# Scaling the residual rows on GpSimd during the up projections, and loading the second half's rows early

## The chip, the cores and the metric

The kernel runs on one NeuronCore of a Trainium2 chip. Its engines work side by side, each through its own queue in order, and wait for one another by semaphores: TensorE (PE in the profile: matrix products, with PEld for the loading of the stationary operand), VectorE (DVE), ScalarE (ACT), GpSimd (POOL) and SyncE (SP, which here only issues transfers). A name with a q (SPq, POOLq) is the queue of an engine, which starts its transfers. The metric is the time of one execution on the device, in microseconds; lower is better.

## The reference

Two layers of a small language-model trunk over a sequence of 1024 tokens of width 1024, in float32. Each layer has a mixer (in the first a gated delta rule, in the second a retention) and a feed-forward part with a gate, and each of the two ends in a residual sum and a layer norm:

```
for i in range(DEPTH):                       # DEPTH = 2
    mod = (e @ ada_w[i] + ada_b[i])[:, None, :]
    sh1, sc1, g1, sh2, sc2, g2 = jnp.split(mod, 6, axis=-1)
    y = mixers[i % N_MIXERS](x * (1.0 + sc1) + sh1)
    x = layer_norm(DN_ALPHA * x + (1.0 + g1) * y, ln_g[i, 0], ln_b[i, 0])
    y = conv_ffn(x * (1.0 + sc2) + sh2, ffn_up[i], ffn_conv_w[i], ffn_conv_b[i], ffn_down[i])
    x = layer_norm(DN_ALPHA * x + (1.0 + g2) * y, ln_g[i, 1], ln_b[i, 1])
return x
```

`e` comes from a conditioning vector. `conv_ffn` has an up projection to twice 2816 columns, a short causal convolution and a gate, and a down projection back to 1024.

What matters for the change: a layer norm is a normalization per row, then a multiplication by a row `ln_g` and the addition of a row `ln_b` (the gain). The sum in front of the second norm needs the first norm's output with its gain.

## The kernel before, in words

*Layout.* A tile has 128 partitions; a row tile holds 128 tokens with 1024 columns (or 512, a half, `HALF`). The sequence is worked on in two halves of 512 tokens, four row tiles each. Matrices are split into a high and a low part (`split`, L88 to L90: ScalarE rounds, VectorE subtracts) and multiplied by three products. Large products use a seven-product scheme over blocks of two by two.

*Rows.* The norm in the middle of a layer writes normalized rows without the gain to a tensor in DRAM, `x_mid` (`xs`); the stores are on ACT's queue (`ln_store`, L372 to L374). The products behind the norm have the gain folded into their scale and shift (`fold`). The residual sum at the layer's end needs the rows with the gain.

*The stages of one layer's end* (`layer_tail`, L1519): in the first layer a projection with norm (`proj_ln`, which loads the layer's input rows `xt<-in_x`, L284); in the second one a seven-product projection (`proj_gen`) does that. Then come the up projections (`strassen`, L1161): 22 items, the first two by a plain scheme (`side`), during which the operands' sums are built (`build_T`, L411, with the transposes of L425 that read the second half's rows), and 20 by seven products (`wino`, L1220). `wino` loads two weight tiles (`wr<-in_ffn_up`, L1223 and L1224), each item about 19 us of TensorE, and calls `bg_step` twice. `bg_step` works off a list of background units: here the products of the conditioning (`bg_ada`: a load `mvw<-in_ada_w`, L215, and behind it multiply-adds on VectorE into `ada`, L225 and L227). The results of a pair of items are stored as `ad<-o` (L1573), partly after sums on GpSimd (L1589). Last is the down projection, again `proj_gen` (L1278): seven products in the order of `prods`, each over `nj` blocks, with loads `ar<-ad` (L1274) and `Br<-in_ffn_down` (L1307) on SP, and results worked off by f1 to f7 and by `finish` and `norm`.

*The gain for the residual rows of the down projection* is made inside `proj_gen`, two ways. For the first half `xload` (L1352) loads the rows without gain in the third product (p == 2), and VectorE multiplies and adds (L1357). For the second half `gain_half` (L1343) does one half row tile in every other step of the fourth and fifth product (p of 3 and 4): SP loads it into one of two buffers with the tag `xT`, GpSimd multiplies and adds (L1349), and a transfer on GpSimd's own queue (L1350) stores it to `xg[i + 1]`. The second half's rows are loaded from there behind the sixth product's work, into the same four `lane` buffers that the first half's rows had. `load_row` waits by `after("w")` for the issue of the last weight block.

*Buffers.* Tags name sets of equal buffers (`BUFS`, L43): `lane` 4, `xT` 2, `auh` 8 of half width (gain rows, gate rows, later trigonometric tables `trig`, L1636), `wr` 2. A tile's load waits until the buffer's last use has ended.

*Order of the work.* The program is written as one stream; a scheduler with a simulated timeline puts each engine's instructions in their order when the program is built. An engine's queue is then worked off strictly in that order: a transfer that waits at the head of SP's queue holds all behind it.

Of the kernel before, what the change touches and what calls it, by code (L numbers as in the profile page):

```python
# [15 lines left out]
P = 128  # L16
# [3 lines left out]
HALF = 512  # L20
# [13 lines left out]
def trunk_kernel(ctx: ExitStack, tc, A):  # L34
# [84 lines left out]
    def bg_step(tile=mm_tile):  # L119
        bg_ps[0] = tile  # L120
        for p in pend:
            p[0] -= 1
        while pend and (pend[0][0] <= 0 or not bg):
            pend.pop(0)[1]()
            if not bg:
                break
        if bg:
            nxt = bg.pop(0)()
            if nxt:
                pend.append(list(nxt))  # L130

    def gemm_feat(src, hT_, step=True):
# [247 lines left out]

    def bg_gain(n, src, dst):
        gb = []

        def unit(c, r):
            if r == 0:
                gb[:] = [tl("auh", [P, HALF], name="gb") for _ in range(2)]
                for t, nm in zip(gb, ("ln_g", "ln_b")):
                    sp.dma_start(t, A[nm][n:n + 1, hs(c)].to_broadcast([P, HALF]))
            x = tl("lane", [P, HALF], name="xg")
            rs = slice(r * P, r * P + P)  # L390
            sp.dma_start(x, src[rs, hs(c)])
            if r == 7:
                return gain(x, rs, c)
            return 1, lambda: gain(x, rs, c)

        def gain(x, rs, c):
            pool.tensor_tensor(x, x, gb[0], ALU.mult)
            pool.tensor_tensor(x, x, gb[1], ALU.add)
            sp.dma_start(dst[rs, hs(c)], x)

        for c in range(2):
            for r in range(8):
                bg.append(lambda c=c, r=r: unit(c, r))

# [756 lines left out]
    def strassen(hT0, xts, scale, shift, items, tags=("hTb", "hTb", "qkv", "qkv", "aux"), direct=False):  # L1161
# [58 lines left out]
        def wino(n, sink):  # L1220
# [27 lines left out]
            sink(2, prod(a22, "T4"), u3)  # L1248
            bg_step()

        bg_tag[0] = "lane"
# [25 lines left out]

    def proj_gen(nj, ablk, wsrc, slots, xsrc, G, final, ln_next, tag, ltags, dst, key, mm=pe.matmul, gate=None, gain=None):  # L1278
        bal = {nm: BAL[ltags[4] + nm] for nm in ABLK + ("w11", "w21", "w22", "wT1", "wT2", "wT3", "wT4", "n", "h")}
# [60 lines left out]
        stats = [[], []]  # L1340
        grows = gain_rows(gain[0], key) if gain else None

        def gain_half(n):  # L1343
            hf, rs = n // 4, slice(HALF + n % 4 * P, HALF + (n % 4 + 1) * P)
            x = tl("xT", [P, HALF], name="xg")
            with after("w"):
                sp.dma_start(x, gain[1][rs, hs(hf)])
            for r, op in zip(grows, (ALU.mult, ALU.add)):
                pool.tensor_tensor(x, x, r[hf], op)  # L1349
            pool.dma_start(xsrc[rs, hs(hf)], x)  # L1350

        def xload(half, t):  # L1352
            xt = load_row(xsrc if half or not gain else gain[1], half, t)
            if half == 0 and gain:
                for r, op in zip(grows, (ALU.mult, ALU.add)):
                    for hf in range(2):
                        dve.tensor_tensor(xt[:, hs(hf)], xt[:, hs(hf)], r[hf], op)  # L1357
            xts[half].append(xt)
            stats[half].append(tl("st", [P, 2, 6]))

        def finish(half, t, nh, c):
            dve.tensor_tensor(c, c, G[nh], ALU.mult)
            xv = xts[half][t][:, hs(nh)]
            dve.scalar_tensor_tensor(xv, xv, ALPHA, c, ALU.mult, ALU.add)
            dve.bn_stats(stats[half][t][:, nh], xv)

        def norm(half, t):
# [7 lines left out]
            else:  # L1375
                (gB, bB), out = final
                r0 = half * HALF + t * P
                dve.scalar_tensor_tensor(mv[:, 2:3], mv[:, 0:1], -1.0, mv[:, 3:4], ALU.mult, ALU.mult)
                lo, hi = xt[:, hs(0)], xt[:, hs(1)]
                act.activation(hi, hi, AF.Identity, bias=mv[:, 2:3], scale=mv[:, 3:4])  # L1380
# [70 lines left out]
        for p, (an, bn, fin, side, fresh) in enumerate(prods):  # L1451
# [8 lines left out]
            for j in range(nj):  # L1460
# [5 lines left out]
                with after("a"):  # L1466
                    for st in steps[p * nj + j + ahead:p * nj + j + ahead + 1]:
                        load_b(*st)
                if gain and p in (3, 4) and j % 2 == 0 and j < 8:
                    gain_half((p - 3) * 4 + j // 2)  # L1470
                if gain and p == 2 and j % 2 == 0 and j < 8:
                    xload(0, j // 2)
                if p == 2 and j < 4 and gate:
                    xload(0, j)
# [29 lines left out]
            if p == 4:  # L1504
                hooks = [] if final else ln_hooks(0, xts[0], tag, ln_next, outs, dst, key, bal["h"])
                hooks += [lambda t=t: xload(1, t) for t in range(4)]
        if not final:
# [11 lines left out]
    def layer_tail(i, mix, wout, xsrc, x_mid, x_out, ln_next, final):  # L1519
# [11 lines left out]
        else:  # L1531
            mix.append((sc2, sh2))
            hT0, xts = proj_st(mix[0])
        bg_ada(i, 5, "row")
        if i == 0:
            for j in (1, 0, 4, 3):
# [6 lines left out]
        def pair_items(fp):  # L1543
# [31 lines left out]
            def up_start():  # L1575
                seen = []

                def gated(q, a, b):
# [7 lines left out]
                    if len(seen) == 4:  # L1586
# [7 lines left out]

        strassen(hT0, xts, sc2, sh2, [it for fp in range(NF // 2) for it in pair_items(fp)])
        slots = {"c": "hTa", "x": "qkv"}
        gb2 = gain_rows(3, ("mid", i), "hTb") if final else None
        return proj_st(proj_gen(NF // 2, ablk_of(ad, "qkv"), A["ffn_down"][i], slots, xg[i + 1], rows[i, 5],
                       (gb2, x_out) if final else None, ln_next, "hTb", ("hTb", "hTa", 8, 6, "f") if final else ("qkv", "hTa", 8, 4, "0"), x_out, ("out", i), gain=(2 * i, x_mid)))

# [357 lines left out]
```

## Time and profile before

Three runs took 2961.66, 2965.21 and 2967.01 us, median 2965.21. The profiled execution took 2955.5 us; its span (first to last instruction) is 2953.7 us, at a granted TensorE clock of 0.984.

| stretch (us) | what | PE busy | DVE busy | POOL busy | granted clock |
|---|---|---|---|---|---|
| 645 to 760 | first layer, projection with norm | 109.10 of 115 | 78.12 | 8.58 | 0.97 |
| 760 to 1195 | first layer, up projections | 428.39 of 435 | 367.73 | 50.28 | 0.99 |
| 1195 to 1425 | first layer, down projection | 218.38 of 230 | 192.87 | 47.19 | 0.99 |
| 2100 to 2290 | second layer, end of the mixer and its projection | 176.93 of 190 | 155.45 | 32.43 | 0.96 |
| 2290 to 2717 | second layer, up projections | 418.74 of 427 | 325.20 | 49.37 | 1.00 |
| 2717 to 2953 | second layer, down projection, end | 215.15 of 236 | 207.55 | 50.19 | 0.97 |

How to read it: "busy" is the time in which an engine worked on instructions; the rest it waited or had nothing to do. PE is the engine that is busy most, so the columns of the others matter where PE is below the stretch's length. The granted clock is the share of full speed that TensorE was given.

### The profile page before, as it was taken

Reading aid. Unit: us, or ns where it says so; the run is one execution under the profiler, and the core shown is the slowest. Engines: PE = TensorE matmul, PEld = TensorE weight load, DVE = VectorE, ACT = ScalarE, POOL = GpSimd, SP = SyncE. Lnnn points to the kernel's source line nnn. Section 1 sums busy time; section 2 is a strip of 40 time slices with the busy share of each in tenths; the row PEclk is TensorE's granted clock in tenths of the full one; section 3 lists DMA queues with packets and bytes.
Section 4 is the critical chain, followed back from the end, with each engine's and each line's share of the span. In section 5 each row is a group of like instructions: output and inputs, shape, how many; then the busy total and the mean of one; then the engine's idle time right before and its main releaser. Section 6 shows DMA issues by size and latency. Waiting matters only on the chain.

```text
span 2953.7 us, 38896 instructions
## 1 busy us (share of the span) xinstructions
PE 2816.4 (95%) x13638; PEld 2303.2 (78%) x13638; DVE 2243.3 (76%) x4005; ACT 1318.0 (45%) x2413; POOL 451.1 (15%) x469
## 2 busy tenths in 40 slices
PE   8998898999999999999999999999999899999997
PEld 7887777887788888877878877777777788888885
DVE  5788787656688888968676756666689787777989
ACT  4745565444544444545333333222244544445443
POOL 0302221100001111140000022422202011111211
PEclk9999999999999999999999999999999999999999
DMA  7231222254244445765343364755654343324763
GB/s 277 86 111 65 83 79 80 83 168 158 92 160 163 150 162 174 286 225 175 131 147 121 109 229 144 222 169 177 198 204 146 103 136 107 107 102 159 278 205 136
DMA packets 244403, 451.01 MB, mean 153 GB/s; under 512 B 23088, under 2 KB 76592, under 8 KB 244208
## 3 DMA queue, kind: packets, MB, share of 16 engines
q1 hardware_dynamic: 213088, 401.07, 41.1%
q10 hardware_dynamic: 29760, 43.00, 4.0%
q0 software_dynamic: 1360, 4.46, 0.4%
q8 instruction: 107, 1.75, 0.2%
q14 instruction: 88, 0.72, 0.1%
HBM read 339.91 MB, written 108.53 MB: 152 GB/s over the span
## 4 chain that ended last, share of the span: by engine, by line
PE 77%; DVE 9%; DMA 6%; ACT 4%; issue 2%; POOL 1%; SPq 0%; POOLq 0%; ACTq 0%; DVEq 0%
PE acc L655 15%; PE acc L1167 10%; PE acc L110 6%; PE acc L111 6%; PE acc L112 6%; PE sc L1167 5%; PE acc L1441 4%; PE sc L655 4%; PE mm L655 2%; PE sc L111 2%; PE sc L112 2%; PE sc L110 2%; PE mm L658 1%; DMA Br<-in_ffn_down 1%; PE acc L314 1%
## 5 line engine op out<-in xcount | busy, mean ns | idle before, releaser
L655 PE MATMUL acc<-hT,wh 128*128 128x512 f32 x960 | 300.1, 394 | 0.0
L1441 PE MATMUL acc<-bb,ab 128*128 128x512 f32 x984 | 233.4, 395 | 9.7 <-DVE bb L90 7.0
L1589 POOL TENSOR_TENSOR o<-o 128x512 f32<-128x512 f32 x80 | 112.3, 1414 | 793.6 <-DVE o L1582 494.0
L1441 PEld LDWEIGHTS acc<-bb,ab 128*128 128x128 f32 x984 | 183.7, 189 | 54.0 <-DVE bb L90 11.8
L1167 PE MATMUL acc<-T,wb 128*128 128x512 f32 x840 | 202.9, 390 | 6.5 <-DVE wb L90 6.5
L655 PEld LDWEIGHTS acc<-hT,wh 128*128 128x128 f32 x960 | 182.2, 190 | 34.1
L89 ACT ACTIVATE ab<-ar 128x512 fp32r<-128x512 f32 x210 | 130.4, 627 | 174.1 <-PE mm L291 57.4
L655 PE MATMUL acc<-hT,wl 128*128 128x512 f32 x480 | 201.2, 419 | 0.0
L1167 PEld LDWEIGHTS acc<-T,wb 128*128 128x128 f32 x840 | 157.0, 188 | 42.9 <-DVE wb L90 9.8
L90 DVE TENSOR_TENSOR wl<-wr,wh 128x1024 fp32r<-128x1024 f32 x95 | 123.3, 1298 | 81.9 <-ACT wh L89 81.6
L90 DVE TENSOR_TENSOR ab<-ar,ab 128x512 fp32r<-128x512 f32 x210 | 159.7, 765 | 30.0 <-ACT ab L89 29.9
L90 DVE TENSOR_TENSOR wb<-mm,wb 128x512 fp32r<-128x512 f32 x216 | 146.0, 684 | 26.4 <-ACT wb L89 25.5
L89 ACT ACTIVATE wh<-wr 128x1024 fp32r<-128x1024 f32 x95 | 100.8, 1062 | 142.8 <-PE acc L655 66.4
L90 DVE TENSOR_TENSOR wb<-wr,wb 128x512 fp32r<-128x512 f32 x162 | 110.5, 687 | 69.0 <-ACT wb L89 68.8
L1228 ACT ACTIVATE pc<-acc 128x512 f32<-128x512 f32 x143 | 84.9, 594 | 163.1 <-PE acc L1167 108.8
L1568 DVE SCALAR_TENSOR_TENSOR o<-g,vc,o 128x512 f32<-128x512 f32 (+2 forms) x176 | 145.6, 844 | 6.2 <-ACT o L1563 5.5
L89 ACT ACTIVATE wb<-mm 128x512 fp32r<-128x512 f32 x216 | 123.9, 595 | 53.8 <-DVE mm L1217 49.3
L89 ACT ACTIVATE wb<-wr 128x512 fp32r<-128x512 f32 x162 | 99.8, 629 | 99.7 <-DMA wr<-in_ffn_up 36.4
L655 PE MATMUL acc<-wh,hT 128*128 128x512 f32 x384 | 137.4, 420 | 2.9 <-DVE vv L90 1.7
L110 PE MATMUL acc<-T,wb 128*128 128x512 f32 x292 | 115.6, 396 | 9.4 <-DVE wb L90 9.4
L476 DVE SCALAR_TENSOR_TENSOR qkv<-raw,vc,qkv 128x512 f32<-128x512 f32 x144 | 111.7, 780 | 11.4 <-ACT qkv L474 10.7
L111 PE MATMUL acc<-T,wb 128*128 128x512 f32 x292 | 115.1, 394 | 0.0
(641 smaller groups left out, 7428.6 us busy)
## 6 DMA issues: line engine op xcount, KB each, us to landing
wr<-in_ffn_up SPq DMA_DIRECT2D x92, 512.0 KB, 4.2
mvw<-in_ada_w SPq DMA_DIRECT2D x80, 512.0 KB, 4.1
ad<-o SPq DMA_DIRECT2D x154, 256.0 KB, 3.1
ar<-ad SPq DMA_DIRECT2D x154, 256.0 KB, 4.8
Br<-in_ffn_down SPq DMA_DIRECT2D x88, 256.0 KB, 4.3
wr<-in_ret_wv SPq DMA_DIRECT2D x32, 512.0 KB, 4.1
ar<-od SPq DMA_DIRECT2D x56, 256.0 KB, 5.4
xs<-xt ACTq DMA_DIRECT2D x24, 512.0 KB, 3.6
```

The costliest lines, as they stand in the source:

```text
L89: act.activation(dst_h, src, AF.Copy)
L90: eng.tensor_tensor(dst_l, src, dst_h, ALU.subtract)
L110: mm(acc, wl[:, k], hl[0], start=first, stop=False)
L111: mm(acc, wh[:, k], hl[1], start=False, stop=False)
L112: mm(acc, wh[:, k], hl[0], start=False, stop=last)
L476: dve.scalar_tensor_tensor(oh, raw[:, 3 - j:515 - j], w[:, 3 - j:4 - j], oh, ALU.mult, ALU.add)
L655: pq(pe.matmul(out, lhsT, rhs, start=start, stop=stop), cost)
L1167: return pe.matmul(*a, skip_group_check=True, **kw)
L1228: act.activation(t, X, AF.Copy)
L1441: return pe.matmul(*args, skip_group_check=True, **kw)
L1568: dve.scalar_tensor_tensor(tv, gv[:, c0 - j:c1 - j], w[:, 2 - j:3 - j], tv, ALU.mult, ALU.add)
L1589: (dve if fp == 0 else pool).tensor_tensor(o[d], o[x], o[y], op)
```

## The change

Both halves' rows are now scaled by one helper, `bg_gain`, that existed for another place. For the rows of the down projections it puts 16 units (two column halves, eight row tiles each) on a list of its own, `rowq`; `row_step`, called at the end of each `wino`, finishes the unit loaded before (GpSimd multiplies and adds, and stores through its own queue) and starts the next load, into the `xT` buffers. What is left of the list is worked off behind `strassen`. `gain_half` and VectorE's multiplications and additions in `xload` go. The gain rows of one column half are two `auh` tiles where four were held before.

Second, the second half's rows: the first two row tiles go to the two `xT` buffers instead of `lane`; in the last projection (`final`) the other two go to pairs of `auh` tiles, and all four are loaded during the fourth product (p == 3). `xh` picks a column half from either kind of tile. The mixer's projection in the second layer (`gate`) has the `xT` part of this too.

```diff
--- before.py
+++ after.py
@@ -128,6 +128,16 @@
             nxt = bg.pop(0)()
             if nxt:
                 pend.append(list(nxt))
+
+    rowq, rowp = [], []
+
+    def row_step():
+        if rowp:
+            rowp.pop()()
+        if rowq:
+            nxt = rowq.pop(0)()
+            if nxt:
+                rowp.append(nxt[1])
 
     def gemm_feat(src, hT_, step=True):
         w = load_w(src)
@@ -378,7 +388,7 @@
 
     xg = [dr.tile([S, D], F32, tag=f"xg{i}", name=f"xg{i}") for i in range(3)]
 
-    def bg_gain(n, src, dst):
+    def bg_gain(n, src, dst, tag="lane"):
         gb = []
 
         def unit(c, r):
@@ -386,7 +396,7 @@
                 gb[:] = [tl("auh", [P, HALF], name="gb") for _ in range(2)]
                 for t, nm in zip(gb, ("ln_g", "ln_b")):
                     sp.dma_start(t, A[nm][n:n + 1, hs(c)].to_broadcast([P, HALF]))
-            x = tl("lane", [P, HALF], name="xg")
+            x = tl(tag, [P, HALF], name="xg")
             rs = slice(r * P, r * P + P)
             sp.dma_start(x, src[rs, hs(c)])
             if r == 7:
@@ -396,11 +406,11 @@
         def gain(x, rs, c):
             pool.tensor_tensor(x, x, gb[0], ALU.mult)
             pool.tensor_tensor(x, x, gb[1], ALU.add)
-            sp.dma_start(dst[rs, hs(c)], x)
+            (sp if tag == "lane" else pool).dma_start(dst[rs, hs(c)], x)
 
         for c in range(2):
             for r in range(8):
-                bg.append(lambda c=c, r=r: unit(c, r))
+                (bg if tag == "lane" else rowq).append(lambda c=c, r=r: unit(c, r))
 
     def ln_hooks(half, xts, tag, vecs2, out, dst, key, npool=0):
         def build(f):
@@ -1247,6 +1257,7 @@
             sink(3, X, z5)
             sink(2, prod(a22, "T4"), u3)
             bg_step()
+            row_step()
 
         bg_tag[0] = "lane"
         for n in range(2):
@@ -1275,7 +1286,7 @@
             return raw
         return ablk
 
-    def proj_gen(nj, ablk, wsrc, slots, xsrc, G, final, ln_next, tag, ltags, dst, key, mm=pe.matmul, gate=None, gain=None):
+    def proj_gen(nj, ablk, wsrc, slots, xsrc, G, final, ln_next, tag, ltags, dst, key, mm=pe.matmul, gate=None):
         bal = {nm: BAL[ltags[4] + nm] for nm in ABLK + ("w11", "w21", "w22", "wT1", "wT2", "wT3", "wT4", "n", "h")}
         pa = [tl("aux", [P, 2, HALF], name="pa") for _ in range(4)]
         p1 = [pa[t // 2][:, t % 2] for t in range(4)]
@@ -1338,29 +1349,28 @@
 
         xts = [[], []]
         stats = [[], []]
-        grows = gain_rows(gain[0], key) if gain else None
-
-        def gain_half(n):
-            hf, rs = n // 4, slice(HALF + n % 4 * P, HALF + (n % 4 + 1) * P)
-            x = tl("xT", [P, HALF], name="xg")
-            with after("w"):
-                sp.dma_start(x, gain[1][rs, hs(hf)])
-            for r, op in zip(grows, (ALU.mult, ALU.add)):
-                pool.tensor_tensor(x, x, r[hf], op)
-            pool.dma_start(xsrc[rs, hs(hf)], x)
 
         def xload(half, t):
-            xt = load_row(xsrc if half or not gain else gain[1], half, t)
-            if half == 0 and gain:
-                for r, op in zip(grows, (ALU.mult, ALU.add)):
-                    for hf in range(2):
-                        dve.tensor_tensor(xt[:, hs(hf)], xt[:, hs(hf)], r[hf], op)
-            xts[half].append(xt)
+            if half and t < 2:
+                x = load_row(xsrc, half, t, tag="xT")
+            elif half and final:
+                x = two("auh", F32, "xt")
+                r0 = HALF + t * P
+                for hf in range(2):
+                    with after("w"):
+                        sp.dma_start(x[hf], xsrc[r0:r0 + P, hs(hf)])
+            else:
+                x = load_row(xsrc, half, t)
+            xts[half].append(x)
             stats[half].append(tl("st", [P, 2, 6]))
+
+        def xh(half, t, nh):
+            x = xts[half][t]
+            return x[nh] if isinstance(x, tuple) else x[:, hs(nh)]
 
         def finish(half, t, nh, c):
             dve.tensor_tensor(c, c, G[nh], ALU.mult)
-            xv = xts[half][t][:, hs(nh)]
+            xv = xh(half, t, nh)
             dve.scalar_tensor_tensor(xv, xv, ALPHA, c, ALU.mult, ALU.add)
             dve.bn_stats(stats[half][t][:, nh], xv)
 
@@ -1376,7 +1386,7 @@
                 (gB, bB), out = final
                 r0 = half * HALF + t * P
                 dve.scalar_tensor_tensor(mv[:, 2:3], mv[:, 0:1], -1.0, mv[:, 3:4], ALU.mult, ALU.mult)
-                lo, hi = xt[:, hs(0)], xt[:, hs(1)]
+                lo, hi = xh(half, t, 0), xh(half, t, 1)
                 act.activation(hi, hi, AF.Identity, bias=mv[:, 2:3], scale=mv[:, 3:4])
                 dve.scalar_tensor_tensor(lo, lo, mv[:, 0:1], gB[0], ALU.subtract, ALU.mult)
                 dve.scalar_tensor_tensor(lo, lo, mv[:, 3:4], bB[0], ALU.mult, ALU.add)
@@ -1466,10 +1476,10 @@
                 with after("a"):
                     for st in steps[p * nj + j + ahead:p * nj + j + ahead + 1]:
                         load_b(*st)
-                if gain and p in (3, 4) and j % 2 == 0 and j < 8:
-                    gain_half((p - 3) * 4 + j // 2)
-                if gain and p == 2 and j % 2 == 0 and j < 8:
+                if not gate and p == 2 and j % 2 == 0 and j < 8:
                     xload(0, j // 2)
+                if final and p == 3 and j % 2 == 0 and j < 8:
+                    xload(1, j // 2)
                 if p == 2 and j < 4 and gate:
                     xload(0, j)
                     finish(0, j, 0, c11[j])
@@ -1503,7 +1513,8 @@
                 yield "P2"
             if p == 4:
                 hooks = [] if final else ln_hooks(0, xts[0], tag, ln_next, outs, dst, key, bal["h"])
-                hooks += [lambda t=t: xload(1, t) for t in range(4)]
+                if not final:
+                    hooks += [lambda t=t: xload(1, t) for t in range(4)]
         if not final:
             for t in range(4):
                 ln_store(1, t, xts[1], dst, key)
@@ -1532,6 +1543,7 @@
             mix.append((sc2, sh2))
             hT0, xts = proj_st(mix[0])
         bg_ada(i, 5, "row")
+        bg_gain(2 * i, x_mid, xg[i + 1], "xT")
         if i == 0:
             for j in (1, 0, 4, 3):
                 bg_ada(1, j, "col")
@@ -1593,10 +1605,12 @@
             return [(up[4 * fp], up[4 * fp + 2], gate_start, conv), (up[4 * fp + 1], up[4 * fp + 3], up_start, None)]
 
         strassen(hT0, xts, sc2, sh2, [it for fp in range(NF // 2) for it in pair_items(fp)])
+        while rowq or rowp:
+            row_step()
         slots = {"c": "hTa", "x": "qkv"}
         gb2 = gain_rows(3, ("mid", i), "hTb") if final else None
         return proj_st(proj_gen(NF // 2, ablk_of(ad, "qkv"), A["ffn_down"][i], slots, xg[i + 1], rows[i, 5],
-                       (gb2, x_out) if final else None, ln_next, "hTb", ("hTb", "hTa", 8, 6, "f") if final else ("qkv", "hTa", 8, 4, "0"), x_out, ("out", i), gain=(2 * i, x_mid)))
+                       (gb2, x_out) if final else None, ln_next, "hTb", ("hTb", "hTa", 8, 6, "f") if final else ("qkv", "hTa", 8, 4, "0"), x_out, ("out", i)))
 
     g1 = two("auh", F32, "g1")
     for nh in range(2):
```

## The prediction

> **What bounds the kernel now.** I read the page first (busy shares, then the forty slices), next the tensor engine's waits and busy time by stage, then the chain of waits through the worst stage, and last the timelines of the places where the change puts its work.
>
> ```profile
> span 2953.7 us, 38896 instructions
> PE 2816.4 (95%) x13638; PEld 2303.2 (78%) x13638; DVE 2243.3 (76%) x4005; ACT 1318.0 (45%) x2413; POOL 451.1 (15%) x469
> ```
>
> PE is busy 95% of the span, so work taken from another engine gains only where PE waits for it, and work put on another engine costs only where PE comes to wait. One stage where it waits is the first layer's down projection:
>
> ```profile
> 1225.00:1255.00 30.00, 30.00 (x134) 24.85 (x133) 30.00 (x51) 15.02 (x27) 1.86 (x1) 1.00 0.75 273
> 1285.00:1315.00 30.00, 30.00 (x134) 24.73 (x132) 14.13 (x17) 13.15 (x24) 13.65 (x12) 1.00 0.83 290
> 1315.00:1345.00 30.00, 23.02 (x96) 18.78 (x95) 26.95 (x45) 6.95 (x13) 0.00 (x0) 0.89 0.60 191
> ```
>
> Columns of this view: stretch, length, busy time (instructions) of PE, PEld, DVE, ACT and POOL, then granted clock, DMA share, GB/s. From 1315 PE loses 7 us, and the clock falls to 0.89. The waits of PE and the chain say why:
>
> ```profile
> PE sc L289 <- DVE u L1414: 7.0, 1, 7.0
> ```
> ```profile
> 1283.60 5.80 DMA xg<-xs
> ...
> 1292.88 3.98 DMA xg<-xg
> ...
> 1296.91 3.44 DMA xg<-xs
> ...
> 1309.54 5.14 DMA Br<-in_ffn_down
> ```
>
> The row loads of `gain_half` have two buffers. The load at 1296.91 had to wait until the store of an earlier row (1292.88, 3.98 us) had landed; it stood at the head of SP's queue, and the weight block `Br` behind it came too late. One buffer's cycle, load to next load, was 1296.91 - 1283.60 = 13.3 us here.
>
> **The change part by part.**
>
> *Removed from the down projections.* Sixteen VectorE multiplications and additions per layer (L1357) and the eight half rows of `gain_half`, each with a load on SP, two POOL operations and a store on POOL's queue.
>
> ```profile
> L1357 DVE TENSOR_TENSOR xt<-xt,rowb x32: 677/681/686, 1234.6 to 2781.2; 128x512 f32<-128x512 f32 x32
> ```
>
> 32 x 0.681 = 21.8 us leave VectorE, but where they stand (1225 to 1255 above) PE is busy 30.00 of 30: I take 0 (the cover is PE itself; without it, half of this per layer). The SP queue of the down projections no longer holds a load that waits for a buffer, so the 7.0 us wait goes, and with it the slow restart, 30 x (1 - 0.89) = 3.3 us: -10.3. Bounds: -7.0 if the clock dips elsewhere, -13 if the waits for VectorE just after it go too.
>
> *Added to the up projections: where the rows really stand.* The source puts one row behind each seven-product unit, but the built order of the changed program does not spread them. In the first layer SP's order is:
>
> ```
> xg 1, xg 2, wr, wr, xg 3, wr, xg 4, xt<-in_x x4, ... xg 5, xg 6, wr, xg 7, xg 8, trig, xg 9, trig,
> xg 10, xg 11, wr(L1223), xg 12, wr(L1224), xg 13 to 16, mvw, trig x2, ad x4, wr(L1223), ...
> ```
>
> All sixteen loads stand ahead of the first `mvw` (a block of the conditioning weights) of the up projections. In the second layer it is xg 1 to 4, the first pair's weights, xg 5 to 8, `mvw`, and the rest mixed with the second and third pairs' weights. SP takes its queue in order, and two buffers serve all rows; so whatever stands behind row n waits for row n - 2 to be loaded, scaled and stored. The price of a row, by the nearest rows:
>
> ```profile
> L1349 POOL TENSOR_TENSOR xg<-xg,rowb x32: 1280/1604/8602, 1253.1 to 2833.2; 128x512 f32<-128x512 f32 x32
> ```
> ```profile
> L1347 SPq DMA_DIRECT2D xg<-xs x16: 319/372/435, 1250.1 to 2828.1; - x16
> ...
> DMA to landing us min/median/max: 2.9/3.3/6.1
> ```
> ```profile
> L1350 POOL DMA_DIRECT2D xg<-xg x16: 559/582/759, 1263.7 to 2834.8; - x16
> ...
> DMA to landing us min/median/max: 2.4/3.2/5.4
> ```
> ```profile
> mvw<-in_ada_w SPq DMA_DIRECT2D x80, 512.0 KB, 4.1
> ...
> xs<-xt ACTq DMA_DIRECT2D x24, 512.0 KB, 3.6
> ```
>
> In the first layer POOL's order puts one operation of the partner row ahead of each store, so a cycle of a pair of rows is load 3.3 + three operations 4.8 + about 0.3 before the issue + landing 3.2 = 11.6 us. Bounds: all minima, 2.9 + 3.8 + 0.3 + 2.4 = 9.4; the cycle seen in the chain, 13.3.
>
> ```profile
> 755.57 0.33 ACTq L374 DMA_DIRECT2D xs<-xt  x1
> ```
> ```profile
> 791.30 0.38 SPq L215 DMA_DIRECT2D mvw<-in_ada_w  x1
> ```
> ```profile
> 811.01 0.48 DVE L225 TENSOR_SCALAR ada<-mvw,e 128x512 f32<-128x512 f32 x1
> ```
> ```profile
> 817.12 2.10 PE L1167 MATMUL acc<-T,wb 128*128 128x512 f32 x8 [0.49 <-DVE wb L90]
> ```
>
> Row 5 is the first of the second half: its source is stored at 755.57 and lands 3.6 us later, 759.2. Row 15 is five cycles behind, 759.2 + 58.0 = 817.2; row 16 one operation and one issue later, 819.4; then `mvw`, 819.7, which lands at 823.8. Before, `mvw` was issued at 791.30 and had long landed when VectorE read it at 811.01 (L225). VectorE's order at this place is the same in both programs, so it would stand at L225 until 823.8, 12.8 us. Behind it on VectorE are the splits (`wb`, L90) for which PE waits already at 817.12: nothing covers it, **+12.8**. Bounds by the same sum: with 9.4 us +1.8, with 13.3 us +21.3. The delay of the first pair's weights (row 11 at 794, against 788.33 before) and of the next pair's fall inside this wait.
>
> In the second layer the two buffers hold normalized rows until their last transposes:
>
> ```profile
> 2303.36 1.03 PE L425 MATMUL mm<-cst,xt 128*128 128x128 f32 x8
> ```
> ```profile
> 2319.59 0.60 SPq L215 DMA_DIRECT2D mvw<-in_ada_w  x1
> ```
> ```profile
> 2339.32 0.48 DVE L225 TENSOR_SCALAR ada<-mvw,e 128x512 f32<-128x512 f32 x1
> ```
>
> Row 1 can load at 2304.4. POOL's order here has the four operations of a pair ahead of both stores: 3.3 + 6.4 + 0.3 + 3.2 = 13.2 us a cycle (bounds 10.7 and 14.9, as above with one operation more). Row 7 loads at 2304.4 + 39.6 = 2344.0, row 8 at 2344.6, `mvw` at 2345.0, landed at 2349.1 against 2339.32: **+9.8** (bounds +2 and +15; the upper end rises by 7 if the third pair's weights, behind row 14, are late too).
>
> *The stores on POOL's queue.* 32 instead of 16, 0.58 us each on POOL, which has 85% free; inside the cycles above. The Trainium skill warns of such stores (SBUF — State Buffer, "SBUF: two separate sides"): a DMA issued from GpSimd can starve for descriptors while VectorE runs an instruction in a two-port mode. The trace's 16 stores landed in 2.4 to 5.4 us beside a busy VectorE, which does not look like it. By the rows the cycle is 11.6 us, by the rule it would be longer by what a starved store adds, and this would count eight times.
>
> *Row loads in the first `proj_ln`.* Rows 3 and 4 now stand ahead of `xt<-in_x`, which VectorE already awaits:
>
> ```profile
> 720.90 1.75 SPq L284 DMA_DIRECT2D xt<-in_x  x4
> ```
> ```profile
> 724.65 0.69 DVE L346 SCALAR_TENSOR_TENSOR xt<-xt,t 128x512 f32<-128x512 f32 x1 [0.33 <-DMA xt<-in_x]
> ```
>
> Both wait for the stores of rows 1 and 2, which end about one cycle after the first half's own stores. VectorE has no slack there (it waited 0.33 for the data), so I take +1, and as bounds 0 and the landing of one row load, +3.
>
> *Early second-half rows.* In the last projection they no longer wait for buffers of the first half:
>
> ```profile
> 2925.51 1.65 SPq L284 DMA_DIRECT2D xt<-xg  x3
> ```
> ```profile
> 2924.87 0.69 DVE L1364 SCALAR_TENSOR_TENSOR xt<-xt,pa 128x512 f32<-128x512 f32 x1 [1.10 <-issue]
> ...
> 2929.49 0.69 DVE L1364 SCALAR_TENSOR_TENSOR xt<-xt,pa 128x512 f32<-128x512 f32 x1 [0.98 <-DMA xt<-xg]
> ```
>
> VectorE ends the kernel, with little idle: what goes is 1.10 + 0.98 = -2.1. Bounds: 0 if the order finds no other work, -6 if the four L1364 and four L1365 (0.69 each) move wholly into earlier gaps. In the other two projections two of four rows come early; I take -0.5 (0 to -1).
>
> **Sum.** -10.3 + 12.8 + 9.8 + 1 - 2.1 - 0.5 = +10.7 us. The profiled execution took 2955.5 us (span 2953.7), 9.7 below the median of 2965.21: 2966 for one like it, **2976** on the scale of the median.
>
> **The rivals.**
>
> *Faster: the rows keep ahead of their readers.* If the pair cycle C is short, both `mvw` land in time. Late are 5C - 45.2 in the first layer and 3(C + 1.6) - 29.8 in the second; with the other terms (-11.9) the sum is zero at C = 10.3 us. At the minima (9.4) it is -11.9 + 1.8 + 2 = -8: 2957. For it: the DMA share is low there, and POOL has nothing else. Against it: VectorE is dense in this stretch, and POOL's operations beside a dense VectorE took up to 8.6 us.
>
> *No change.* C near 10.3, or one of the two waits covered: 2965.
>
> *Slower still: POOL holds VectorE.* An operation of POOL lengthens VectorE's:
>
> ```profile
> 1262.21 1.78 DVE L90 TENSOR_TENSOR bb<-Bw,bb 128x512 fp32r<-128x512 f32 x1
> ```
> ```profile
> 2370.00:2450.00 80.00, 79.49 (x346) 64.44 (x346) 64.00 (x97) 36.39 (x62) 10.72 (x8) 1.00 0.41 132
> ```
>
> A tensor-tensor operation of this size took 0.68 us above, 1.1 less. At 1.1 us for each of 32 operations a layer that is 35 us; VectorE has 16 us free in 80, some 18 in the 90 us that the rows take. If half of the remaining 17 reaches PE in each layer: +17, 2993. In the sum I charge nothing for it, since most operations fall where VectorE reads PSUM or stands at L225.
>
> *Slower still: starved stores.* Landings of 5.4 instead of 3.2 us would lengthen eight cycles by 2.2: +17.6, 2994. The rule quoted above would do this.
>
> **How the numbers follow.** Two executions of this kernel differ by about 0.2% (6 us), what a measurement can tell from no change. Forecast 0.55, faster rival 0.15, no change 0.19, POOL holding VectorE 0.07, starved stores 0.04. The forecast's own range, from half of the two waits to both upper ends, is 2964 to 2990, and a tenth of it lies within 0.2%, with as much of the slower rivals beyond. So faster 0.15, same 0.2, slower 0.65. The range that leaves out 2 in 10 runs from the faster rival to the two slower ones: 2957 to 2993.
>
> **What would show it.** Right: in the profile after, VectorE waits some 10 us for `mvw` at L225 near 811 and again near 2340, with PE idle behind it; SP waits for row stores; the 7.0 us wait for L1414 is gone, and the tail has no wait for `xt<-xg`. Wrong: row 16 issued before about 807 and row 8 before 2335 (a pair cycle near 9 us), or VectorE with other work at that place; then the gains stand alone. It would also be wrong if L1414 waits again without the rows, since the 10.3 us would then belong to something else.

## The result

The changed kernel takes 2981.99 us (median of 4 runs, 2979.15 to 2983.88), the kernel before 2963.43 us (2953.2 to 2967.01) beside it: ratio 1.0062, 95% interval 1.0042 to 1.0081. It is slower by 18.6 us, and the forecast of 2976 was 6 us low. The range and the sign hold; the reasons hold only in part.

```profile
span 2982.1 us, 38985 instructions
PE 2829.5 (95%) x13638; PEld 2311.5 (78%) x13638; DVE 2242.9 (75%) x3973; ACT 1317.4 (44%) x2413; POOL 502.2 (17%) x517
```

VectorE has 32 instructions less and GpSimd 48 more. VectorE's busy time is nevertheless the same (2243.3 before), though 32 x 0.681 = 21.8 us of its work are gone: something lengthened the rest.

Both traces have the same matrix products in nearly the same order, so the start of each can be compared with its start before. The change of that difference over a stage of the kernel before is what the stage lost or gained:

| stage (us of the kernel before) | gained or lost (us) | forecast |
|---|---|---|
| 0 to 645 | +0.9 | 0 |
| 645 to 760, projection with norm | +1.8 | +1 |
| 760 to 1195, first layer's up projections | +13.7 | +12.8 |
| 1195 to 1425, first layer's down projection | -2.9 | -10.3 |
| 1425 to 2290, second layer's mixer | +1.2 | -0.5 |
| 2290 to 2717, second layer's up projections | +20.0 | +9.8 |
| 2717 to TensorE's last product | -2.9 | 0 |
| behind it | -3.3 | -2.1 |

The sum, 28.5, is the difference of the two spans up to rounding. That is more than the 18.6 of the medians, because the profiled execution of before lay 8 us under its median and that of after 2 us over; no stage shows where those 10 us are, and below medians decide. A stage read from one pair of traces is uncertain by several us: 1425 to 2290, which the runs below hardly touch, lies between 6.7 us gained (e3) and 10.0 lost (e8).

In each of the two large losses there is one long wait of TensorE, 12.7 and 11.1 us where before it was 4.7. (A line of waits gives the total in us, the number and the longest.) In the first layer 8.1 of the 13.7 us are lost there, 4.0 ahead of it (smaller waits, and a granted clock of 0.94 from 760 to 790 where before it was 1.00) and 1.6 behind. In the second 6.2 of the 20.0 are lost there, 4.3 ahead and 9.5 behind. In the windows (columns as in the prediction), 790 to 826 and 2350 to 2365 are those places, 826 to 860 and 2365 to 2400 the stretches behind them, 1301 to 1331 the one where the 7.0 us were lost before, and 1385 to 1418 the end of the first down projection. The second block has the four places of the up projections in the kernel before:

```profile
PE acc L110 <- DVE wb L90: 23.8, 2, 12.7
PE acc L1451 <- DVE bb L90: 10.7, 11, 3.7
```
```profile
790.00:826.00 36.00, 21.73 (x93) 16.94 (x92) 34.82 (x37) 15.46 (x25) 25.93 (x23) 0.88 0.50 168
826.00:860.00 34.00, 33.51 (x136) 26.98 (x137) 31.52 (x51) 17.00 (x29) 0.00 (x0) 0.92 0.51 171
...
2350.00:2365.00 15.00, 3.92 (x17) 2.96 (x16) 14.93 (x17) 6.75 (x11) 10.73 (x9) 0.73 0.30 105
2365.00:2400.00 35.00, 29.68 (x107) 22.72 (x107) 34.74 (x44) 15.37 (x26) 18.18 (x17) 0.84 0.67 220
...
1301.00:1331.00 30.00, 30.00 (x134) 24.86 (x133) 18.37 (x29) 13.37 (x24) 0.00 (x0) 1.00 0.61 186
...
1385.00:1418.00 33.00, 27.10 (x118) 21.37 (x118) 29.50 (x49) 24.05 (x44) 0.59 (x1) 0.90 0.44 160
```
```profile
787.00:811.00 24.00, 18.62 (x81) 14.66 (x79) 21.67 (x32) 13.77 (x24) 0.00 (x0) 0.97 0.20 67
811.00:845.00 34.00, 33.36 (x135) 26.91 (x136) 31.43 (x52) 17.28 (x30) 0.00 (x0) 0.92 0.52 171
...
2328.00:2340.00 12.00, 7.31 (x31) 5.75 (x30) 11.29 (x19) 6.76 (x11) 0.00 (x0) 0.95 0.00 0
2340.00:2370.00 30.00, 28.37 (x120) 23.02 (x119) 28.67 (x46) 16.07 (x27) 0.00 (x0) 0.96 0.51 172
```

Behind the first wait the granted clock is the same as before (0.92), behind the second it is lower (0.84 against 0.96). VectorE is busy 34.82 of 36 us in the stretch that ends with TensorE's first long wait. It does not stand waiting for `mvw`. The timeline of the changed kernel around the wait, and below it the landing of that `mvw` (view of line L225):

```profile
817.18 0.39 SPq L225 DMA_DIRECT2D mvw<-in_ada_w  x1
...
819.75 5.40 DVE L1580 SCALAR_TENSOR_TENSOR o<-g,vc,o 128x512 f32<-128x512 f32 x5
825.07 0.68 DVE L90 TENSOR_TENSOR wb<-mm,wb 128x512 fp32r<-128x512 f32 x1
825.67 0.47 DVE L235 TENSOR_SCALAR ada<-mvw,e 128x512 f32<-128x512 f32 x1
...
825.80 0.79 PE L110 MATMUL acc<-T,wb 128*128 128x512 f32 x1 [12.75 <-DVE wb L90]
```
```profile
DMA to landing us min/median/max: 4.3/4.3/4.3
```

`mvw` was as late as forecast (817.18, forecast 819.7) and landed at 821.5. But VectorE came to L235 (L225 before) only at 825.67, with no idle time ahead of it, and the split `wb` that released TensorE stands before L235. The data were there first. What was late was VectorE itself, by work that had become longer. In the second layer it is the same: `mvw` was issued at 2358.42 (forecast 2345.0, and 14.6 us had been lost by then), VectorE came to L235 at 2364.48 and did not wait. The groups by line of the dense stretch (number, then busy us and mean ns of one, then idle us before them), VectorE before (758 to 816), and VectorE and GpSimd after (760 to 830):

```profile
L90 DVE TENSOR_TENSOR T<-bt,T 128x512 fp32r<-128x512 f32 x16 | 10.6, 687 | 6.2 <-ACT T L89 6.2
...
L454 DVE TENSOR_TENSOR bt<-bt,mm 128x512 f32<-128x512 f32 x4 | 2.7, 682 | 0.0
```
```profile
L90 DVE TENSOR_TENSOR T<-bt,T 128x512 fp32r<-128x512 f32 x16 | 16.2, 1041 | 3.4 <-ACT T L89 3.4
...
L464 DVE TENSOR_TENSOR bt<-bt,mm 128x512 f32<-128x512 f32 x4 | 2.7, 679 | 0.0
```
```profile
L408 POOL TENSOR_TENSOR xg<-xg,gb 128x512 f32<-128x512 f32 x12 | 19.2, 1600 | 0.9
L407 POOL TENSOR_TENSOR xg<-xg,gb 128x512 f32<-128x512 f32 x12 | 16.5, 1375 | 20.0 <-DMA xg<-xs 19.9
```

The same sixteen operations took 1041 ns instead of 687. The five L1580 above took 5.40 us; before, as five L1568, 3.39. Operations that read one input from PSUM (`mm`) did not change. Compared one by one, VectorE's operations between 760 and 830 are 16.8 us longer than before, beside 35.7 us of GpSimd's multiplications and additions (24 of the first layer's 32). Of the sixteen `T<-bt,T`, the nine that overlap one of these took 1322 ns on average, the seven others 680, about as before. The Trainium skill has this rule (SBUF — State Buffer, "Who interferes with whom"): a VectorE instruction with two SBUF inputs contends with a GpSimd instruction that reads SBUF, one with at most one SBUF input does not, outside VectorE's two-port modes. The trace agrees on both halves, 687 to 1041 ns and 682 to 679. One operation with a single tile from SBUF, L235 at 2364.48, did take 0.89 us beside GpSimd's instead of 0.48; whether it ran in such a mode no run shows.

### The profile page after: what moved, and what is told of

Same layout as the page of the kernel before. It is cut to its first block, busy times and chain, and to the rows that moved or that the text cites. A ratio compares the mean times of both kernels' runs of the same rounds, so it can differ in the third digit from the quotient of the medians.

```text
span 2982.1 us, 38985 instructions
## 1 busy us (share of the span) xinstructions
PE 2829.5 (95%) x13638; PEld 2311.5 (78%) x13638; DVE 2242.9 (75%) x3973; ACT 1317.4 (44%) x2413; POOL 502.2 (17%) x517
## 4 chain that ended last, share of the span: by engine, by line
PE 69%; DVE 15%; DMA 7%; ACT 4%; issue 3%; POOL 1%; SPq 0%; ACTq 0%; DVEq 0%; POOLq 0%
PE acc L665 15%; PE acc L1177 9%; PE acc L110 5%; PE acc L111 5%; PE acc L112 5%; PE sc L1177 4%; PE sc L665 4%; PE acc L1451 3%; PE mm L665 3%; PE sc L111 2%; PE sc L110 2%; PE sc L112 2%; DVE o L1580 1%; PE mm L668 1%; PE mm L1451 1%
## 5 line engine op out<-in xcount | busy, mean ns | idle before, releaser
L1451 PE MATMUL acc<-bb,ab 128*128 128x512 f32 x984 | 235.7, 397 | 11.9 <-DVE bb L90 10.7
L1177 PE MATMUL acc<-T,wb 128*128 128x512 f32 x840 | 203.2, 391 | 8.4 <-DVE wb L90 8.3
L90 DVE TENSOR_TENSOR ab<-ar,ab 128x512 fp32r<-128x512 f32 x210 | 148.8, 714 | 64.6 <-ACT ab L89 64.6
L90 DVE TENSOR_TENSOR wl<-wr,wh 128x1024 fp32r<-128x1024 f32 x95 | 125.4, 1321 | 83.9 <-ACT wh L89 83.7
L90 DVE TENSOR_TENSOR wb<-wr,wb 128x512 fp32r<-128x512 f32 x162 | 115.1, 715 | 70.3 <-ACT wb L89 69.6
L90 DVE TENSOR_TENSOR wb<-mm,wb 128x512 fp32r<-128x512 f32 x216 | 145.6, 682 | 27.4 <-ACT wb L89 26.6
L1580 DVE SCALAR_TENSOR_TENSOR o<-g,vc,o 128x512 f32<-128x512 f32 (+2 forms) x176 | 152.0, 881 | 5.4 <-ACT o L1575 4.8
L407 POOL TENSOR_TENSOR xg<-xg,gb 128x512 f32<-128x512 f32 x48 | 68.0, 1421 | 474.9 <-DMA xg<-xs 451.2
L110 PE MATMUL acc<-T,wb 128*128 128x512 f32 x292 | 116.4, 399 | 23.9 <-DVE wb L90 23.8
L486 DVE SCALAR_TENSOR_TENSOR qkv<-raw,vc,qkv 128x512 f32<-128x512 f32 x144 | 111.6, 779 | 11.2 <-ACT qkv L484 10.5
```

Source lines behind the costliest of these rows:

```text
L90: eng.tensor_tensor(dst_l, src, dst_h, ALU.subtract)
L110: mm(acc, wl[:, k], hl[0], start=first, stop=False)
L486: dve.scalar_tensor_tensor(oh, raw[:, 3 - j:515 - j], w[:, 3 - j:4 - j], oh, ALU.mult, ALU.add)
L1177: return pe.matmul(*a, skip_group_check=True, **kw)
L1451: return pe.matmul(*args, skip_group_check=True, **kw)
L1580: dve.scalar_tensor_tensor(tv, gv[:, c0 - j:c1 - j], w[:, 2 - j:3 - j], tv, ALU.mult, ALU.add)
```

## The experiments

Theory P: GpSimd's row operations lengthen VectorE's. Theory Q, the forecast's: rows at the head of SP's queue make `mvw` and the weights late. The first four runs set them against each other. Medians stand against the kernel before on the same chip, with the 95% interval of the ratio; stage losses are against the trace of before, as in the table above.

**e1_pool_queue**, P without Q.

```diff
-            sp.dma_start(x, src[rs, hs(c)])
+            (sp if tag == "lane" else pool).dma_start(x, src[rs, hs(c)])
```

> The row loads are issued on GpSimd's queue instead of SP's; the two GpSimd operations a row and everything else stay. Theory P (GpSimd's operations lengthen VectorE's): nothing changes at the two dense places, the split operations T<-bt,T keep a mean near 1.0 us against 0.69 before, TensorE's waits for VectorE of 12.7 and 11.1 us at L110 stay within 2 us, and the time is 2972 to 2984. Theory Q (rows at the head of SP's queue hold weights and mvw back): both long waits fall back to the 4.7 us of before, and the time is about 2982 - 12 - 20 = 2950. Both at once: in between, and mvw issued near 791 shows that the queue no longer takes part.

2982.44 us, 1.0062 (1.0044 to 1.0081): the time of the changed kernel, 2981.99. `mvw` is issued at 800.09 and VectorE never waits for it, but the lengthening is there (first line, groups 760 to 835) and so is the wait of TensorE (second line, 780 to 870):

```profile
L90 DVE TENSOR_TENSOR T<-bt,T 128x512 fp32r<-128x512 f32 x16 | 15.6, 1008 | 2.9 <-ACT T L89 2.9
```
```profile
PE acc L110 <- DVE wb L90: 12.3, 1, 12.3
```

The up projections lose 18.5 and 17.7 us, in a trace whose execution lay 10 us over this run's median. P alone carries the whole loss.

**e3_hops**, Q without P (for the rows with tag `xT` alone).

```diff
-            pool.tensor_tensor(x, x, gb[0], ALU.mult)
-            pool.tensor_tensor(x, x, gb[1], ALU.add)
+            if tag == "lane":
+                pool.tensor_tensor(x, x, gb[0], ALU.mult)
+                pool.tensor_tensor(x, x, gb[1], ALU.add)
+            else:
+                pool.dma_start(dst[rs, hs(c)], x)
+                pool.dma_start(x, dst[rs, hs(c)])
             (sp if tag == "lane" else pool).dma_start(dst[rs, hs(c)], x)
```

> GpSimd's multiplications and additions of the rows are left out (the residual rows lack their gain); in their place each row makes two more trips, store to DRAM and load back, on GpSimd's queue, so that a buffer is held about as long and SP's queue is blocked as before: mvw should be issued near 820 us in the first layer. Theory P: T<-bt,T goes back to 0.69 us and TensorE's long waits to 4.7 us, time about 2950. Theory Q: mvw is late as in the changed kernel, VectorE stands idle at L235 some 10 us, TensorE's waits stay at 11 to 13 us, and the time is 2976 to 2986.

2975.86 us, 1.0048 (1.003 to 1.0066); the up projections lose 13.2 and 22.9 us. VectorE's operations are back at 688 ns, though GpSimd issues three transfers a row here: what lengthened them is GpSimd's arithmetic and not its transfers. Now the wait of the forecast appears at L235, 9.90 us. Groups, VectorE's and TensorE's waits (780 to 870), and timeline:

```profile
L90 DVE TENSOR_TENSOR T<-bt,T 128x512 fp32r<-128x512 f32 x16 | 10.6, 688 | 6.0 <-ACT T L89 5.8
```
```profile
DVE ada L235 <- DMA mvw<-in_ada_w: 9.9, 1, 9.9
...
PE acc L1181 <- DVE wb L90: 10.5, 1, 10.5
PE acc L110 <- DVE wb L90: 4.7, 1, 4.7
```
```profile
817.94 0.39 SPq L225 DMA_DIRECT2D mvw<-in_ada_w  x1
...
822.43 0.49 DVE L235 TENSOR_SCALAR ada<-mvw,e 128x512 f32<-128x512 f32 x1 [9.90 <-DMA mvw<-in_ada_w]
```

So Q would carry a loss of this size too. (In the second layer the held loads show elsewhere: VectorE waited 2.2 us for `mvw`, but ScalarE 13.1 for one `ad<-o`.) In the changed kernel both run side by side: VectorE, lengthened, reaches L235 after the late `mvw` has landed. The two delays did not add up: in the first layer P alone cost 18.5 us, Q alone 13.2, both together 13.7. Taking one of them away brought nothing in e1 and 6 us in e3.

**e6_no_arith**, neither P nor the long cycle (again for `xT` alone).

```diff
-            pool.tensor_tensor(x, x, gb[0], ALU.mult)
-            pool.tensor_tensor(x, x, gb[1], ALU.add)
+            if tag == "lane":
+                pool.tensor_tensor(x, x, gb[0], ALU.mult)
+                pool.tensor_tensor(x, x, gb[1], ALU.add)
```

> The changed kernel with GpSimd's multiplications and additions of the rows left out (the residual rows lack their gain) and nothing in their place: a row's cycle falls to about 3.3 + 0.3 + 3.2 = 6.8 us, so mvw should be issued near 797 us, land near 801, and be in time for VectorE. With neither the lengthening nor the late mvw, the up projections should be as before: about 2982 - 14 - 20 = 2948 to 2956. If the 32 more transfers cost something by themselves, above 2960.

2961.8 us, 0.9996 (0.9982 to 1.001): 20 us under the changed kernel, but over the expected 2948 to 2956. The shorter cycle does not free SP's queue enough: the first layer's weights are issued at 798.21 instead of 788.33 (+5.0 us in the up projections), and in the second layer `mvw` leaves at 2345.13 and VectorE waits for it (+11.3). VectorE's waits, 2310 to 2420:

```profile
DVE ada L235 <- DMA mvw<-in_ada_w: 9.4, 1, 9.4
```

So in the second layer, where the buffers come free late, Q is there even at this shortest cycle.

**e4_vector**, the arithmetic on VectorE.

```diff
-            pool.tensor_tensor(x, x, gb[0], ALU.mult)
-            pool.tensor_tensor(x, x, gb[1], ALU.add)
+            (pool if tag == "lane" else dve).tensor_tensor(x, x, gb[0], ALU.mult)
+            (pool if tag == "lane" else dve).tensor_tensor(x, x, gb[1], ALU.add)
```

> The rows' multiplications and additions are on VectorE instead of GpSimd, at the same places: 32 x 0.68 = 21.8 us more VectorE work a layer, no GpSimd operation beside it. Theory P: VectorE loses about as much to its own work as it lost by being lengthened (16.8 us in the first layer), so the long waits stay and the time is 2972 to 2990. Theory Q: a row's cycle falls to 3.3 + 1.4 + 0.3 + 3.2 = 8.2 us, mvw comes in time, and the time is 2952 to 2965.

2987.0 us, 1.0085 (1.0058 to 1.0113), stages +13.1 and +23.0. VectorE's operations have their old length (686 ns), but it has the rows' work as well. In the first layer the rows' 32 operations take 21.8 us of VectorE; in the changed kernel VectorE's own operations are 22.1 us longer over all sixteen rows (690 to 840 us), so handing them to GpSimd at this place saved VectorE nothing. `mvw` was again issued late (819.34, so the cycle did not fall as Q had it), and VectorE waited only 0.4 us for it.

**e2_one_per_item**, the rows spread.

```diff
-            sp.dma_start(x, src[rs, hs(c)])
+            with after("item" if tag != "lane" else None):
+                sp.dma_start(x, src[rs, hs(c)])
...
-            sp.dma_start(wb, ub)
+            anchor["item"] = sp.dma_start(wb, ub)
```

> Each row load is tied behind the issue of its own item's weights, so that rows come one per item (some 19 us apart) instead of all at once; the work is the same. Both theories expect the +13.7 us of the first and the +20 us of the second layer's up projections to go: 2946 to 2954. If the rows cost VectorE time wherever they stand (32 operations a layer, 1.1 us each, part of it reaching TensorE), it stays above 2962.

2964.2 us, 1.001 (0.9994 to 1.0026). Both theories had expected 2946 to 2954. The long waits are gone, but the up projections still lose 10.8 and 6.4 us, in small pieces. One stretch far from the dense places, before and spread (in the second, 98.01 of 100):

```profile
963.00:1060.00 97.00, 97.00 (x435) 80.36 (x434) 82.80 (x131) 47.18 (x99) 16.76 (x12) 1.00 0.51 168
```
```profile
970.00:1070.00 100.00, 98.01 (x433) 79.54 (x432) 86.63 (x130) 46.45 (x99) 35.00 (x28) 1.00 0.58 189
```

Compared one by one, VectorE's operations in the first layer's up projections are 13.5 us longer than before. With VectorE 86% busy, 16 rows cost 10.8 us, 0.7 each. GpSimd's 85% of free time was not free.

**e5_before_pool_queue** and **e9_every_third** test the forecast's first step in the kernel before, by one small edit each.

```diff
-                sp.dma_start(x, gain[1][rs, hs(hf)])
+                pool.dma_start(x, gain[1][rs, hs(hf)])
```

> The kernel before, with one edit: the loads of gain_half are issued on GpSimd's queue instead of SP's, so that no load waiting for a buffer stands at the head of SP's queue in the down projections. If the forecast's first step holds (-7.0 of wait, -3.3 of clock), the time is 2953. If TensorE only comes earlier to a place where VectorE is the bound, as the changed kernel's trace has it (-10.0 at the wait, +6.8 behind it), it is 2958 to 2962. No gain at all (2963 or more) if the wait was due to something else than SP's order.

2957.57 us, 0.9982 (0.9967 to 0.9996), between the expected 2953 and 2958 to 2962. The down projection gains 10.5 us, the step's own number. The up projections lose 8.0 and 5.6: on GpSimd's queue nothing held the eight rows back, and the scheduler put them into the dense stretch. Timeline of GpSimd, the first and the last of these rows:

```profile
765.99 3.01 POOL L1349 TENSOR_TENSOR xg<-xg,rowb 128x512 f32<-128x512 f32 x2 [2.95 <-DMA xg<-xs]
...
805.19 2.99 POOL L1349 TENSOR_TENSOR xg<-xg,rowb 128x512 f32<-128x512 f32 x2 [0.25 <-DMA xg<-xs]
```

VectorE's operations between 690 and 840 are 12.7 us longer than before. This is theory P once more, without any change to the up projections' own work.

```diff
-                if gain and p in (3, 4) and j % 2 == 0 and j < 8:
-                    gain_half((p - 3) * 4 + j // 2)
+                if gain and p in (3, 4) and j % 3 == 0:
+                    gain_half((p - 3) * 4 + j // 3)
```

> The kernel before, with gain_half in every third step of the fourth and fifth product instead of every other one: a row each 8.1 us (three steps of twelve products at 0.226 us) instead of 5.4, and a buffer's cycle of 13.3 us over two buffers is 6.7. If the wait of 7.0 us came from the rows at the head of SP's queue, it goes with nothing else touched: -7 to -10.5, 2953 to 2957. If it comes from the weights' own transfers, the wait stays and the time with it, 2963.

2950.98 us, 0.9952 (0.9934 to 0.9969), under the expected 2953 to 2957: faster than both kernels, the 7.0 us wait gone, nothing moved. The down projection gains only 4.1 us in its trace, since another wait (5.9 us for `bb`) appears behind; the rest of the 12.7 us is spread (3.8 us between 1425 and 2100 the largest), and its cause is open.

**e8_no_early_rows** and **e12_first_layer_late** undo the second part, everywhere and in the first layer's down projection alone.

```diff
-            if half and t < 2:
+            if half and t < 2 and (final or gate):
```

(This is e12's edit; in e8, not shown, `xload` is `load_row(xsrc, half, t)` throughout, behind the sixth product.)

> The changed kernel without its second part: the second half's rows of the two down projections and of the mixer's projection are loaded into the lane buffers behind the sixth product, as before. By the forecast's step for the early rows (-2.1, -0.5) the time rises to about 2985. If the early loads are what costs the 6.8 us at the end of the first layer's down projection, it falls to 2977 to 2980.

> The changed kernel with the early second-half rows taken back in the first layer's down projection alone (both other places keep them). Forecast's step for them (-0.5 for two of four rows early): nothing to see, 2982, and TensorE's wait of 3.7 us at the end of that projection stays. If the two early rows are what gave 6.8 us back there: that stage gains 8 to 10 us on the kernel before instead of 3, and the time is 2975 to 2978.

e8: 2978.52 us, 1.0051 (1.0031 to 1.0071). e12: 2977.74 us, 1.0052 (1.0033 to 1.0071). The medians lie 3 to 4 us under the changed kernel's, the intervals overlap. The stage tells more: the first down projection gains 9.1 and 8.7 us, with early rows 2.9, and 2.1 to 4.9 in the five other traces of the changed kernel's variants that have them (e1 to e4, e6). The timeline of VectorE in the changed kernel, then in e12:

```profile
1382.52 0.69 DVE L1332 TENSOR_TENSOR Br<-Br,Bw 128x512 f32<-128x512 f32 x1
1385.37 0.69 DVE L1332 TENSOR_TENSOR Br<-Br,Bw 128x512 f32<-128x512 f32 x1 [2.15 <-DMA Br<-in_ffn_down]
1387.97 0.69 DVE L1332 TENSOR_TENSOR Br<-Br,Bw 128x512 f32<-128x512 f32 x1 [1.91 <-DMA Br<-in_ffn_down]
1388.58 0.68 DVE L90 TENSOR_TENSOR bb<-Br,bb 128x512 fp32r<-128x512 f32 x1
```
```profile
1382.14 0.69 DVE L1332 TENSOR_TENSOR Br<-Br,Bw 128x512 f32<-128x512 f32 x1 [1.05 <-DMA Br<-in_ffn_down]
1382.75 1.29 DVE L90 TENSOR_TENSOR bb<-Br,bb 128x512 fp32r<-128x512 f32 x2
```

With early rows the built order has three sums of weights in a row, two of them waiting for transfers, ahead of the split `bb` that TensorE waits for (3.7 us at 1389.32); without them a split follows the first sum. That the early rows made the difference is shown; why the scheduler then orders VectorE so is open.

**e7_second_layer, e10_combined, e11_combined_late** look for a version that keeps what works: the rows by GpSimd in the second layer only, one per item from the seventh item on; the first layer as before, with e5's line (e7) or e9's (e10, e11); early rows in the second layer (e7, e10) or none (e11). Two places of these edits, the ones that choose where the rows go:

```diff
             bg_step()
-            row_step()
+            if n >= 6:
+                row_step()
...
-        bg_gain(2 * i, x_mid, xg[i + 1], "xT")
+        if i:
+            bg_gain(2 * i, x_mid, xg[i + 1], "xT")
```

> A candidate: the first layer as in the kernel before with gain_half's loads on GpSimd's queue; in the second layer the rows by GpSimd during the up projections, one load behind each item's weights from the seventh item on, where VectorE is busy 75%, and the second half's rows loaded early. If a row costs nothing there, 2963 - 3 - 3 = 2955 to 2959. If a row costs 0.7 us there, as it did in the first layer when spread (VectorE 86% busy), 11 us more: 2966 to 2970.

> The candidate of before (second layer's rows one per item from the seventh item on, second half's rows early there), with the first layer's rows back on SP, in every third step of its down projection, so that GpSimd no longer scales them beside the dense stretch at 765 to 808 us, where the candidate lost 7.3 us. If that loss was GpSimd's, 2951 - 7 = 2942 to 2947; if not, 2951.

> The same as e10_combined, with the second half's rows loaded late into the lane buffers in both layers and in the mixer, as before. By the forecast's step for the early rows it is 2 to 2.6 us slower than e10_combined. By the trace of e8_no_early_rows, which lost nothing at the kernel's end without early rows, it is the same within 2 us.

e7: 2951.45 us, 0.9959 (0.9945 to 0.9973), under the expected 2955 to 2959. e10: 2953.31, 0.9965 (0.995 to 0.9981). e11: 2953.45, 0.9968 (0.9954 to 0.9983). All are faster than both kernels and none differs from e9 by what can be measured. In the second layer's up projections the 16 rows now cost 1.2, 1.4 and 0.8 us (VectorE about 75% busy there). In e10 VectorE's operations are still 9.8 us longer there than before, but TensorE comes to wait for little of it: where a row stands decides its price. The first layer's up projections lost 8.2 us in e7 and 0.8 in e10, as expected; but e10's down projection gained only 1.6 against 8.5, so the sum is the same, and the expected 2942 to 2947 were missed. e10 and e11 tie. Behind TensorE's last product, the nine profiled kernels with early rows in the last projection gain 2.2 to 4.2 us on before (the changed one 3.3); of the four without (e5, e8, e9, e11) one gains 1.0 and the others 0.2 or nothing. So the early rows do shorten the tail, and in e10 against e11 something else took it back.

## Why the prediction was right or wrong

*Down projections, -10.3.* Right by itself: 10.5 in e5, 9.1 and 8.7 in e8 and e12. In the changed kernel it came to 2.9, for the reason under *Other early rows*. That VectorE's 21.8 us there are worth nothing holds: e5 keeps them and gains the whole.

*First layer's up projections, +12.8; measured +13.7.* The number is right and its reason is wrong, so its closeness is luck: the wait that was forecast would have cost 13.2 by itself (e3), but another delay of that size covered it. All sixteen rows stood ahead of `mvw`, and it left at 817.18, as the sum had it. But "it would stand at L225 until 823.8" did not happen: VectorE was still on its way there. The step that failed is the sentence that charged nothing for GpSimd beside VectorE, "since most operations fall where VectorE reads PSUM or stands at L225". Enough of them fell on splits and sums with both inputs in SBUF: VectorE became 16.8 us longer in the dense stretch, 22.1 over all sixteen rows. The rival "POOL holds VectorE" was the mechanism at work; it got a chance of 0.07 and was priced on top of the waits, where the two overlap (e1, e3). Its own row, 1.78 us for an operation of 0.68, stood in the prediction.

*Second layer's up projections, +9.8; measured +20.0.* The same, and a size missed: VectorE's operations between 2290 and 2450 are 21.3 us longer. TensorE's long wait grew by 6.4 us (11.1 against 4.7). The rest is mostly a wait of 2.6 us for a lengthened `bt` at 2331, waits for splits of the next pairs (1.9 and 3.3 us; before, one of 1.6), and a lower granted clock behind (0.84 in 2365 to 2400, 0.96 before).

*Projection with norm, +1; measured +1.8*, within its bounds, but not by its reason. VectorE did wait 1.5 us for `xt<-in_x` instead of 0.6; in e6 it waited as long, and the stage lost 0.2. In the changed kernel VectorE's operations between 690 and 760 are 5.4 us longer, and TensorE's waits for `t` (L324) rose from 1.9 to 3.5 us.

*Tail, -2.1; measured -3.3* behind TensorE's end. The two waits at L1364 are gone, as forecast. The 2.9 us before it are not the early rows': e5 and e8, without them, gain 2.5 and 3.6 there.

*Other early rows, -0.5.* Wrong: +5.8 (8.7 less 2.9) in the first down projection. The step looked at when data arrive and not at VectorE's order, which the edit also changed.

*Starved stores* did not show: the changed kernel's 32 stores on GpSimd's queue landed at a median of 2.9 us, the longest in 6.8 (before: 3.2 and 5.4). *The rows keep ahead of their readers* did not occur either: e6 shows that even a cycle without arithmetic does not suffice in the second layer.

*The sum.* The stages of the traces add up to 28.5 us where the forecast has 10.7. That 2976 still came within 6 us of the median owes something to luck, since the profiled executions lay 10 us further apart than the medians.

## What to carry to other kernels

An engine that is 15% busy is not free if its operations lengthen those of the engine that TensorE waits for: look at which inputs the neighbour reads at that place, and put the work where that neighbour has slack (0.05 to 0.09 us a row here in e7, e10 and e11, against 0.9 to 1.3 in the changed kernel). Two delays that run side by side need not add up (18.5 and 13.2 us alone, 13.7 together): test each alone before believing a number that fits. When a load that waits for its buffer blocks a queue, first ask for it less often: one edit (every third step instead of every other) brought 12.7 us here, of which the trace of e9 places 4.1 in the down projection it was made for.

## What the runs showed of the hardware

A VectorE operation on 128x512 with both inputs in SBUF took up to 2.33 us (L90 at 2786.39 of the kernel before; mostly up to 1.78) beside GpSimd's tensor-tensor operations instead of 0.69, while one with an input from PSUM kept 0.68; GpSimd's own went from 1.28 up to 2.28 us (L407 in the changed kernel). In the dense stretch of the changed kernel, 35.7 us of GpSimd's arithmetic cost VectorE 16.8 us. The transfers that GpSimd issued in e3 cost VectorE nothing that could be seen.
